# Low parts of the first layer's weight pieces: VectorE alone instead of VectorE and GpSimd by turns

## The chip, the core and the metric

The program runs on one core of one Trainium2 chip. The metric is the device time of that core in microseconds (us), the median of three runs. The engines are called as the profile calls them: PE (TensorE), PEld (its weight loads), DVE (VectorE), ACT (ScalarE), POOL (GpSimd) and SP (SyncE, which here issues most transfers).

## What is computed

The reference is a decoder trunk of two layers on 256 tokens of width 2048, all in float32. Each layer has three parts:

```
h = rmsnorm(x, g_mix_pre)
rq, rk, rv, rg, su, dq, dk, dv = split(h @ w_in)
x += rmsnorm(concat(retention(rq, rk, rv, rg), s5(su), diff_attention(dq, dk, dv)) @ w_out)
x += rmsnorm(cross_attention(rmsnorm(x), rmsnorm(mem)))
x += rmsnorm(square(relu(rmsnorm(x) @ w_up)) @ w_down)
```

The change touches only the first of these lines of the first layer: the products that make rv, rg, rq, rk and su.

## The kernel before

**Split products.** The float32 products are made of matmuls on a rounded format. A weight piece of 128 x 1024 numbers (512 KB) is loaded as `raw`; ACT rounds it into `hi` (L172); the rest, `raw - hi`, is the second part `lo` (L176). The activations `hT` are split in the same way. A product is hi x hi, lo x hi and hi x lo: for the pieces of `w_ina` that is twelve matmuls a piece on L264, L265 and L266, of which L265 reads `lo`; for those of `w_inb` 24 shorter ones on L329, L330 and L331.

**Stages of the first layer.** The projections run in the order RV, RG, RQ, RK (eight pieces each, `proj_A`) and SU (two groups of four pieces, `proj_B`), 40 pieces in all. In the profile RG starts at 43.28 us, SU at 155.2, and the last matmul of SU is out at 197.6. The numbers in tile names rise with the program's order. Piece 1 of RG is hi_459 with lo_460, the last piece of RQ is hi_942 with lo_943, the first of RK hi_977 with lo_978, and SU starts at hi_1265. `raw` has three buffers, `hi` and `lo` five each (`NRAW, NHL = 3, 5`).

**Other work of the same stretch.** While PE goes through these pieces, DVE also makes the parameters of both layers (`params`: L386 to L527, among them the powers and rotations of `cmul`, L473 to L478), the rotation table (L579 to L584), the S5 operands, and the elementwise parts of the projections (L986 to L992 is the rotation of rq and rk, L1053 and L1054 the gate of rg). `s5_setup` makes the S5 operands in eight units. For each unit DVE writes the block `BJ` (L633 to L640) and the block `C5` (L656 to L664); PE transposes BJ (L647, four matmuls) and multiplies by C5 (L672, eight records); ACT copies the results; DVE adds a diagonal (L682). BJ is one buffer in `ws`: DVE may write the next unit's BJ when PE and ACT have read the last one. `t5` uses POOL for integer work (L865).

**Order of the work.** The Tile framework orders each engine's instructions by priority, which is the place in the program, when it builds the kernel; on the chip each engine takes them in that order and waits where an operand is missing. `high_priority(offset=50)` moves an instruction 50 places ahead of its own. In the first layer's stretch up to the end of SU, `lo_pool` is 2 (`LOP = (2, 0)`), so `fetch` gives every second `lo` to POOL; elsewhere it is 0 and all `lo` are on DVE with no offset.

Of the kernel before, what the change touches and what calls it, by code (L numbers as in the profile page):

```python
# [8 lines left out]
F32 = mybir.dt.float32  # L9
# [4 lines left out]
ALU = mybir.AluOpType  # L14
AX = mybir.AxisListType
PSUM = bass.MemoryType.PSUM
DRAM = bass.MemoryType.DRAM

P = 128
# [29 lines left out]
class Trunk:  # L49
    def __init__(self, ctx, tc, ins, out):  # L50
        self.ctx, self.tc, self.nc, self.i, self.out = ctx, tc, tc.nc, ins, out
        self.bg = []
        self.first = None
        self.have = []
        self.count = 0
        self.lo_pool = 0
        self.todo = self.plan()
        self.uid = 0
        self.queue = 0
# [41 lines left out]
    # ------------------------------------------------------------ setup  # L101
# [10 lines left out]
    def rstd(self, out, ss, scale, n):  # L112
        """out[P, n] = (ss * scale + eps) ** -0.5"""
        nc = self.nc
        m = self.tmp.tile([P, 4], F32, tag="tiny", name=self.nm("ms"), bufs=8)
        nc.vector.tensor_scalar(m[:, 0:n], ss, scale, EPS, ALU.mult, ALU.add)  # L116
        nc.gpsimd.tensor_tensor(out=out, in0=m[:, 0:n], in1=self.mhalf[:, 0:n], op=ALU.pow)  # L117
# [5 lines left out]
    # ------------------------------------------------- split helpers  # L123
    def split_act(self, hi, lo, src):
        """hi = f32r(src), lo = f32r(src - hi)"""
        self.nc.scalar.copy(out=hi, in_=src)
        self.nc.vector.tensor_tensor(out=lo, in0=src, in1=hi.bitcast(F32), op=ALU.subtract)

    def plan(self):
        """the weight pieces in the order in which the products take them: (array, index)"""  # L130
        for l in range(L):
            def chunk(n, c, kps, *pre):
                return [(n, (l, *pre, c, k)) for k in kps]
            for c in (C_RV, C_RG, C_RQ, C_RK):
                yield from chunk("w_ina", c, range(8))
            for half in range(2):
                groups = [] if half else [G_SU, G_SU + 1]
                for g in groups + [G_DQ + 2 * half, G_DQ + 2 * half + 1, G_DK + 2 * half, G_DK + 2 * half + 1]:
                    yield from chunk("w_inb", g, range(4))
                yield from chunk("w_ina", C_DV + half, range(8))  # L140
            for ks in (self.KO, self.KD):
                for c in range(2):
                    yield from chunk("w_out", c, ks)
            for c in (2, 3):
                yield from chunk("w_out", c, range(8))
            for n in ("w_xk", "w_xq"):
                for c in range(2):
                    yield from chunk(n, c, range(4))
            yield from chunk("w_xv", 0, range(8))
            for c in range(4):  # L150
                yield from chunk("w_xo", c, range(2))
            for sc in range(4):
                for g in range(8):
                    yield from chunk("w_up", 8 * sc + g, range(4))
                for c in range(4):
                    yield from chunk("w_down", c, range(8), sc)

    def fetch(self):
        """load and split the next weight piece"""
# [3 lines left out]
        src = self.i[key[0]]  # L163
# [7 lines left out]
        with self.tc.high_priority(offset=50 if self.lo_pool else 0):  # L171
            self.nc.scalar.copy(out=hi, in_=raw)  # L172
        self.count += 1
        eng = self.nc.gpsimd if self.lo_pool and self.count % self.lo_pool == 0 else self.nc.vector
        with self.tc.high_priority(offset=50 if self.lo_pool else 0):
            eng.tensor_tensor(out=lo, in0=raw, in1=hi.bitcast(F32), op=ALU.subtract)  # L176
# [12 lines left out]
    def T8(self, slot, shape, dt=F32R, name="t"):  # L189
        """one of the eight 8 KB slots for transposed activations"""  # L190
        return self.tp.tile(shape, dt, tag=f"T{slot}", name=self.nm(name), bufs=1)
# [4 lines left out]
    def scale_split(self, hT, j, ts_, src, gcol):  # L196
        """hT[j][:, :, :, ts_] = f32r parts of src [P, 4, n] times the gain columns"""
# [6 lines left out]
    def from_T(self, hT, srcT, gcol, room=None):  # L204
        """hT from a feature-major input [P, 16, 256]"""
# [7 lines left out]
    def build_T(self, hT, src, t, j, gcol):  # L213
        """hT[j][:, :, :, tok tile t] from src [P tok, 512] times the gain columns"""
# [7 lines left out]
    def after(self, dst, src):  # L222
        """a load into dst starts only when src is there"""
# [6 lines left out]
    def begin(self):  # L230
        """the parameters, and x once its transpose is there"""
# [11 lines left out]
    def x_stat(self, t):  # L243
        """rstd [P, 1] of x tile t"""
# [12 lines left out]
    # ------------------------------------------------- projections  # L257
    def mm_A(self, a, lhs, kp, w, t, first, last):
        """a[tok tile t, 512] += h @ piece kp"""
# [11 lines left out]
    def proj_A(self, lhs, nk, wap, c, sink, arg=None, kps=None, lag=(0, 0)):  # L271
        """acc[tok, 2, 512] = h @ chunk c of w; lag = how many pieces tile 1 runs behind
        tile 0 at the start and at the end (then sink is called per tile)"""
# [33 lines left out]
    def proj_B(self, rhs, nk, wap, c, sink, arg=None, split=False, halves=False):  # L307
        """[P feat, 2 tiles, 256 tok] = group c of w, transposed, times h^T; split: all of token tile 0
        before token tile 1; halves: the products with the two parts of h side by side"""
# [44 lines left out]
    # ------------------------------------------------- trig  # L354
    def sincos(self, ang, n, sn, cs, wk):
        """sn, cs = sin(ang), cos(ang) of [P, n] fp32 angles of any size; wk(k) gives scratch"""
# [25 lines left out]
    def exp_small(self, out, a, wk):  # L382
        """out = exp(a), to fp32 rounding, a clamped to [-87, 88]"""
# [13 lines left out]
    # ------------------------------------------------- parameters of both layers  # L397
    def params(self):
        """rope tables, S5 discretisation (both layers, [P=(2g,64p), 32=(l,pair)])"""
# [19 lines left out]
        if True:  # L419
# [42 lines left out]
            # powers a^0..a^4 of a = mag e^{i th}: pw[P, m, 32]  # L462
# [23 lines left out]
            # unit rotation per chunk of four, and its doublings  # L486
# [11 lines left out]
            # f = (a - 1) / lambda  # L498
# [16 lines left out]
            # lambda of the differential heads  # L515
# [16 lines left out]
    # ------------------------------------------------- S5 operands of one layer, left in DRAM  # L532
# [5 lines left out]
    def s5_setup(self, l, gate=None):  # L538
# [24 lines left out]
        # rotation tables  # L563
# [28 lines left out]
        # B-bar; its imaginary part, like that of the state, is kept negated  # L592
# [11 lines left out]
        # units of two pairs of groups  # L604
# [22 lines left out]
        def stage_a(u):  # L627
            # a^{3-j} B-bar, block-diagonal over the two groups of a pair
# [21 lines left out]
        def stage_x(u):  # L650
            # C a^m, block-diagonal as well
# [14 lines left out]
        def stage_c(u):  # L666
            nc.scalar.copy(out=wtm[u % 2][:, 0:512], in_=pss[u])
            # B C a^m, the same for every j
# [5 lines left out]
        def stage_d(u):  # L674
            # shifted into the lower-triangular block Toeplitz operand; the skip on its diagonal
# [26 lines left out]
    # ------------------------------------------------- S5 group  # L702
    def su_sink(self, acc, arg):
        """[P, 2, 256] -> [P, 2, 4 j, 64 c]"""
# [5 lines left out]
    def s5_relayout(self, suP):  # L710
        """su channel-major -> U4 [(j, 2g, 16h), pair, chunk]"""
# [9 lines left out]
    def s5_main(self, l, st):  # L721
# [52 lines left out]
        def emit(u):  # L774
# [8 lines left out]
            # gelu (tanh form)  # L783
# [22 lines left out]
        # back to channel-major: gF[(q,2g,16h), ft, (i, c)]  # L806
# [34 lines left out]
    # ------------------------------------------------- T5 bias, left in DRAM as 8*bias + mask  # L841
    def t5(self):
        """steps over the bucket edges times the differences of the table's rows"""
# [46 lines left out]
    # ------------------------------------------------- differential heads  # L890
# [11 lines left out]
    def diff_heads(self, l, srcs, yds):  # L902
# [64 lines left out]
        # head -> tick of its four steps  # L967
# [9 lines left out]
    # ------------------------------------------------- retention  # L977
# [78 lines left out]
    # ------------------------------------------------- residual after a sub-layer  # L1056
    def post_sink(self, acc, arg, t0, t1):
        """y*g into self.y, partial sums of squares"""
# [13 lines left out]
    def residual(self, t, rfix=None):  # L1072
        """x tile t += y*g*rstd(y)"""
# [29 lines left out]
    def stat_of(self, t, gate=None):  # L1103
        """1 / rms of x tile t"""
# [7 lines left out]
    def row_of(self, dst, cols):  # L1112
        """dst[P, 256] = the two columns [P, 1] along the free axis of every partition"""
# [9 lines left out]
    # ------------------------------------------------- memory  # L1123
# [15 lines left out]
    # ------------------------------------------------- cross attention  # L1139
# [4 lines left out]
    def scaled(self, acc, arg):  # L1144
        """times a row [P, 256] that is the same on all partitions"""
# [66 lines left out]
    def proj_xo(self, l, xyT):  # L1212
        """four chunks of two pieces; tile 1 runs behind tile 0"""
# [20 lines left out]
    # ------------------------------------------------- MLP  # L1234
# [42 lines left out]
    # ------------------------------------------------- one layer  # L1277
    def layer(self, l, hT):
# [6 lines left out]
        self.lo_pool = self.LOP[l]  # L1285
        self.nt = tk[0]
        with ExitStack() as mx:
# [44 lines left out]
            self.lo_pool = 0  # L1332
# [17 lines left out]
            with ExitStack() as df:  # L1350
# [8 lines left out]
                # out-projection of the first two chunks over what is ready  # L1359
# [70 lines left out]
    LOP = (2, 0)  # L1430
# [55 lines left out]
def layouts(x):  # L1486
    """the inputs laid out as the program reads them, and arrays that depend on the shapes alone"""
# [6 lines left out]
    def tile_a(w):  # L1494
        # [..., K, N] -> [..., N/512, K/256, 128, 2, 512]
# [5 lines left out]
    def tile_b(w):  # L1501
        # [..., K, N] -> [..., N/256, K/512, 128, 4, 256]
# [21 lines left out]
    # persistent small things  # L1524
# [9 lines left out]
    # parameters that only the set-up reads  # L1534
# [12 lines left out]
    # S5: b [(g p), re/im, pair, h], c [(g p), re/im, pair, h]  # L1547
# [32 lines left out]
```

## Time and profile before

| what | us |
|---|---|
| median of three runs (2574.57 to 2579.67) | 2578.06 |
| span of the profiled execution | 2586.3 |
| PE busy in the span | 2494.8 |
| DVE busy | 1631.0 |
| ACT busy | 1226.0 |
| POOL busy | 179.7 |

The profile gives the profiled execution by its span, first to last instruction; a time of that same execution around the span is not given. The span is 8.2 us (0.32%) above the median of the runs. The share of busy time is an average over stages; the stretch from 43 to 198 us is where the change lies, and its own rows stand further down. A row's duration runs to the end of the instruction, which overlaps with the start of the next one; the cost of an instruction on a busy engine is the step from its start to the next start.

### The profile page before, as it was taken

How to read it: one execution, taken by the hardware profiler on the slowest of the kernel's cores; microseconds unless marked ns; L12 is line 12 of the kernel's file. 1: busy time of each engine (PE TensorE's matmuls, PEld its weight loads, DVE VectorE, ACT ScalarE, POOL GpSimd, SP SyncE). 2: the span in 40 equal slices, each digit the busy share in tenths (PEclk: the TensorE clock that was granted, in tenths of full speed). 3: DMA queues.
4: the chain of work that ended last, by engine and by line, in shares of the span. 5: the costliest groups of instructions: out<-in, count | busy, mean ns of one | idle time of the engine just before them, and what ended most of it. 6: DMA issues, size and time to landing. Idle time of an engine off the chain costs nothing.

```text
span 2586.3 us, 36202 instructions
## 1 busy us (share of the span) xinstructions
PE 2494.8 (96%) x13696; PEld 2143.4 (83%) x13696; DVE 1631.0 (63%) x2688; ACT 1226.0 (47%) x1936; POOL 179.7 (7%) x202
## 2 busy tenths in 40 slices
PE   6789999999999999999999999999999999999998
PEld 4588877898888888888878999879788888888886
DVE  8876766657876655555566586656665555555555
ACT  5443456656554434434445435556554444443443
POOL 3433310001000000000000001000000000000000
PEclk9889999999999999999999999999999999999999
DMA  6556665655666665566566555575465556656554
GB/s 247 190 193 190 212 190 166 210 173 172 214 215 212 187 195 187 187 195 187 188 201 197 178 182 177 171 223 177 132 196 193 189 187 195 188 187 195 187 188 146
DMA packets 145630, 491.49 MB, mean 190 GB/s; under 512 B 15744, under 2 KB 28032, under 8 KB 144176
## 3 DMA queue, kind: packets, MB, share of 16 engines
q1 hardware_dynamic: 139904, 470.47, 57.1%
q0 software_dynamic: 4976, 17.14, 2.1%
q8 instruction: 107, 1.75, 0.3%
q10 hardware_dynamic: 576, 1.57, 0.2%
q14 instruction: 67, 0.55, 0.1%
HBM read 469.20 MB, written 19.92 MB: 189 GB/s over the span
## 4 chain that ended last, share of the span: by engine, by line
PE 83%; DVE 7%; DMA 4%; issue 2%; ACT 2%; POOL 1%; SPq 0%; POOLq 0%; DVEq 0%; ACTq 0%
PE acc L326 18%; PE acc L264 13%; PE acc L266 13%; PE acc L265 13%; PE acc L327 9%; PE acc L329 3%; PE acc L330 3%; PE acc L331 3%; DVE lo L176 1%; DMA raw<-in_w_out_dram 1%; PE sm L218 1%; ACT hi L172 1%; DMA raw<-in_w_ina_dram 1%; DMA raw<-in_w_xk_dram 1%; PE sm L750 1%
## 5 line engine op out<-in xcount | busy, mean ns | idle before, releaser
L176 DVE TENSOR_TENSOR lo<-raw,hi 128x1024 fp32r<-128x1024 f32 x795 | 976.2, 1229 | 766.2 <-ACT hi L172 762.4
L172 ACT CAST hi<-raw 128x1024 fp32r<-128x1024 f32 x816 | 857.4, 1051 | 1089.2 <-PE acc L266 465.4
L326 PE MATMUL acc<-hm,hi 128*128 128x512 f32 x1984 | 700.2, 398 | 0.0
L327 PE MATMUL acc<-hm,lo 128*128 128x256 f32 x1984 | 557.0, 281 | 0.0
L326 PEld LDWEIGHTS acc<-hm,hi 128*128 128x128 f32 x1984 | 372.6, 188 | 91.3
L264 PE MATMUL acc<-hi,uT 128*128 128x512 f32 x1024 | 400.4, 391 | 1.6 <-DVE y L1252 1.6
L266 PE MATMUL acc<-hi,uT 128*128 128x512 f32 x1024 | 398.7, 389 | 0.0
L265 PE MATMUL acc<-lo,uT 128*128 128x512 f32 x1024 | 398.6, 389 | 0.0
L327 PEld LDWEIGHTS acc<-hm,lo 128*128 128x128 f32 x1984 | 374.8, 189 | 0.2
L264 PEld LDWEIGHTS acc<-hi,uT 128*128 128x128 f32 x1024 | 192.3, 188 | 41.8 <-DVE y L1252 2.4
L266 PEld LDWEIGHTS acc<-hi,uT 128*128 128x128 f32 x1024 | 192.2, 188 | 40.2
L265 PEld LDWEIGHTS acc<-lo,uT 128*128 128x128 f32 x1024 | 192.3, 188 | 39.2
L329 PE MATMUL acc<-hT,hi 128*128 128x256 f32 x640 | 185.2, 289 | 0.0
L330 PE MATMUL acc<-hT,hi 128*128 128x256 f32 x640 | 183.4, 287 | 0.0
L331 PE MATMUL acc<-hT,lo 128*128 128x256 f32 x640 | 183.2, 286 | 0.0
L265 PE MATMUL acc<-lo,hT 128*128 128x512 f32 x384 | 158.0, 411 | 15.5 <-POOL lo L176 7.9
L264 PE MATMUL acc<-hi,hT 128*128 128x512 f32 x384 | 157.9, 411 | 10.9 <-ACT hi L172 10.6
L266 PE MATMUL acc<-hi,hT 128*128 128x512 f32 x384 | 156.5, 408 | 3.6 <-DVE hT L202 3.6
L117 POOL TENSOR_TENSOR rs<-ms,mhalf 128x1 f32<-128x1 f32 x26 | 18.8, 725 | 1698.0 <-DVE ms L116 993.6
L330 PEld LDWEIGHTS acc<-hT,hi 128*128 128x128 f32 x640 | 123.9, 194 | 1.4
L329 PEld LDWEIGHTS acc<-hT,hi 128*128 128x128 f32 x640 | 123.5, 193 | 1.6 <-issue 1.0
L331 PEld LDWEIGHTS acc<-hT,lo 128*128 128x128 f32 x640 | 123.5, 193 | 1.5 <-issue 0.7
(403 smaller groups left out, 3191.9 us busy)
## 6 DMA issues: line engine op xcount, KB each, us to landing
raw<-in_w_up_dram SPq DMA_DIRECT2D x256, 512.0 KB, 3.5
raw<-in_w_down_dram SPq DMA_DIRECT2D x256, 512.0 KB, 3.5
raw<-in_w_ina_dram SPq DMA_DIRECT2D x96, 512.0 KB, 4.2
raw<-in_w_inb_dram SPq DMA_DIRECT2D x80, 512.0 KB, 4.1
raw<-in_w_out_dram SPq DMA_DIRECT2D x64, 512.0 KB, 4.2
pp<-s5d SPq DMA_DIRECT2D x16, 640.0 KB, 5.2
raw<-in_w_xk_dram SPq DMA_DIRECT2D x16, 512.0 KB, 4.2
raw<-in_w_xq_dram SPq DMA_DIRECT2D x16, 512.0 KB, 4.0
```

The source lines that it names most:

```text
L172: self.nc.scalar.copy(out=hi, in_=raw)
L176: eng.tensor_tensor(out=lo, in0=raw, in1=hi.bitcast(F32), op=ALU.subtract)
L218: nc.tensor.transpose(ps[:, q * P:(q + 1) * P], src[:, q * P:(q + 1) * P], self.ident)
L264: self.nc.tensor.matmul(a, lhsT=xh, rhs=hi[:, kk, :], start=first and kk == 0, stop=False)
L265: self.nc.tensor.matmul(a, lhsT=xh, rhs=lo[:, kk, :], start=False, stop=False)
L266: self.nc.tensor.matmul(a, lhsT=xl, rhs=hi[:, kk, :], start=False, stop=last and kk == 1)
L326: nc.tensor.matmul(acc[:, t, :], lhsT=hi[:, kk, cs], rhs=h, start=(k == 0), stop=False)
L327: nc.tensor.matmul(a, lhsT=lo[:, kk, cs], rhs=h[:, 0, :], start=False, stop=(k == nk - 1))
L329: nc.tensor.matmul(a, lhsT=hi[:, kk, cs], rhs=h[:, 0, :], start=(k == 0), stop=False)
L330: nc.tensor.matmul(a, lhsT=hi[:, kk, cs], rhs=h[:, 1, :], start=False, stop=False)
L331: nc.tensor.matmul(a, lhsT=lo[:, kk, cs], rhs=h[:, 0, :], start=False, stop=(k == nk - 1))
L750: nc.tensor.matmul(bu[:, r, a * 64:(a + 1) * 64], lhsT=win[:, a, r, :], rhs=U4[:, 2 * u + a, :], start=True, stop=True)
```

## The change

In the first layer, from RV to the end of SU, every `lo` is made on DVE. The flag `lo_pool` with its period becomes the flag `rush`, which only sets the priority: the offset of 50 stays for both halves of the split, now under one `with`. Comments and docstrings are blank lines or gone, so line numbers of the changed kernel are lower by 4 or 5 (L172 there is L176 here); below, in the text, all lines are those of the kernel before.

```diff
@@ __init__
-        self.count = 0
-        self.lo_pool = 0
+        self.rush = False
@@ fetch
-        with self.tc.high_priority(offset=50 if self.lo_pool else 0):
+        with self.tc.high_priority(offset=50 if self.rush else 0):
             self.nc.scalar.copy(out=hi, in_=raw)
-        self.count += 1
-        eng = self.nc.gpsimd if self.lo_pool and self.count % self.lo_pool == 0 else self.nc.vector
-        with self.tc.high_priority(offset=50 if self.lo_pool else 0):
-            eng.tensor_tensor(out=lo, in0=raw, in1=hi.bitcast(F32), op=ALU.subtract)
+            self.nc.vector.tensor_tensor(out=lo, in0=raw, in1=hi.bitcast(F32), op=ALU.subtract)
@@ layer
-        self.lo_pool = self.LOP[l]
+        self.rush = l == 0
...
-            self.lo_pool = 0
+            self.rush = False
@@ constants
-    LOP = (2, 0)
```

The scheduler sees the new engine, so the order of the rest moves too. Two places show it.

On DVE, at the first pieces of RG. Lines L473 to L478 (before) and L366 to L373 (change; there they are L370 to L377 of the kernel before) are parameter work. Before:

```order
L176 TENSOR_TENSOR lo_460<-raw_457,hi_459 128x1024
L473 TENSOR_TENSOR par_152<-pwr 128x32
L474 TENSOR_TENSOR par_152<-pwi 128x32
L475 TENSOR_TENSOR pwr<-par_152 128x32
L476 TENSOR_TENSOR par_152<-pwr,pwi 128x32
L477 TENSOR_TENSOR par_152<-pwi,pwr 128x32
L478 TENSOR_TENSOR pwi<-par_152 128x32
L473 TENSOR_TENSOR par_152<-pwr 128x32
L474 TENSOR_TENSOR par_152<-pwi 128x32
L176 TENSOR_TENSOR lo_535<-raw_532,hi_534 128x1024
```

With the change:

```order
L172 TENSOR_TENSOR lo_460<-raw_457,hi_459 128x1024
L368 TENSOR_TENSOR par_152<-par_152 128x160
L369 CAST par_152<-par_152 128x160
L172 TENSOR_TENSOR lo_495<-raw_492,hi_494 128x1024
L370 TENSOR_TENSOR par_152<-par_152 128x160
L371 SCALAR_TENSOR_TENSOR angb<-par_152 128x160
L172 TENSOR_TENSOR lo_535<-raw_532,hi_534 128x1024
```

lo_495, which POOL made before, now stands between its neighbours on DVE, and all three stand ahead of parameter work that they followed before.

On PE, around the first piece of RK. Before (sm_1035 is the transpose of the fourth S5 unit; those of the first three, sm_810, sm_885 and sm_960, stand further up, among the pieces of RQ):

```order
L266 MATMUL acc_757<-hi_942,hT_102 128x512
L647 MATMUL sm_1035<-pk,ws_598 128x128 x4
L264 MATMUL acc_757<-hi_942,hT_102 128x512
L265 MATMUL acc_757<-lo_943,hT_102 128x512
L266 MATMUL acc_757<-hi_942,hT_102 128x512
L264 MATMUL acc_757<-hi_942,hT_102 128x512
L265 MATMUL acc_757<-lo_943,hT_102 128x512
L266 MATMUL acc_757<-hi_942,hT_102 128x512
L264 MATMUL acc_1064<-hi_977,hT_99 128x512
L265 MATMUL acc_1064<-lo_978,hT_99 128x512
```

With the change (L643 and L668 are L647 and L672 of the kernel before):

```order
L262 MATMUL acc_757<-hi_942,hT_102 128x512
L260 MATMUL acc_1064<-hi_977,hT_99 128x512
L643 MATMUL sm_810<-pk,ws_598 128x128 x4
L668 MATMUL sm_838<-ws_598 128x128 x3
L668 MATMUL sm_838<-ws_598,ws_7_105 128x128
L643 MATMUL sm_885<-pk,ws_598 128x128 x4
L668 MATMUL sm_913<-c_119_772,ws_598 128x128 x3
L668 MATMUL sm_913<-c_119_772,ws_7_105 128x128
L261 MATMUL acc_1064<-lo_978,hT_99 128x512
```

The first two S5 units have moved from the middle of RQ to behind the first matmul of RK, ahead of the first matmul that reads lo_978.

## Rows read from the trace of the kernel before

**Rows 1.** First line of the page: the span.
```profile
span 2586.3 us, 36202 instructions
```

**Rows 2.** Windows: RG up to 68 us, RQ, RK, SU, and the rest.
```profile
core 0: us, PE busy (x) PEld busy (x) DVE busy (x) ACT busy (x) POOL busy (x), PEclk, DMA share, GB/s
43.28:68.00 24.72, 19.09 (x68) 14.64 (x69) 23.53 (x82) 14.08 (x27) 12.56 (x12) 0.86 0.63 228
68.00:100.00 32.00, 22.29 (x87) 16.95 (x85) 23.18 (x70) 13.34 (x24) 18.67 (x8) 0.84 0.51 169
100.00:155.20 55.20, 47.27 (x223) 38.47 (x224) 51.91 (x135) 27.89 (x67) 16.77 (x7) 0.91 0.56 183
155.20:197.60 42.40, 34.08 (x261) 33.65 (x259) 24.57 (x43) 17.30 (x40) 14.63 (x8) 0.88 0.65 220
200.00:2586.00 2386.00, 2343.26 (x12960) 2018.91 (x12960) 1472.77 (x2241) 1127.97 (x1732) 100.63 (x148) 0.99 0.60 188
```

**Rows 3.** Waits of PE up to 250 us: in total, times, longest.
```profile
PE sm L899 <- DVE st L992: 11.7, 2, 8.3
PE acc L265 <- POOL lo L176: 7.9, 2, 6.9
PE acc L265 <- DVE lo L176: 5.9, 4, 3.7
PE sm L647 <- DVE ws L639: 4.2, 2, 2.2
PE sm L1120 <- DVE ws L635: 2.8, 1, 2.8
```

**Rows 4.** Timeline of PE around 85 us: start, duration, instruction.
```profile
85.35 0.63 PE L266 MATMUL acc<-hi,hT 128*128 128x512 f32 x1
85.78 0.63 PE L264 MATMUL acc<-hi,hT 128*128 128x512 f32 x1
...
91.05 0.39 PE L265 MATMUL acc<-lo,hT 128*128 128x512 f32 x1
91.28 0.39 PE L266 MATMUL acc<-hi,hT 128*128 128x512 f32 x1
```

**Rows 5.** Groups of POOL: the low parts made there.
```profile
L176 POOL TENSOR_TENSOR lo<-raw,hi 128x1024 fp32r<-128x1024 f32 x21 | 61.3, 2922 | 80.2 <-ACT hi L172 69.2 <-DVE ws L635 5.8 <-PE sm L672 5.2
```

**Rows 6.** Timeline of POOL: two of its 21 low parts.
```profile
15.08 2.37 POOL L176 TENSOR_TENSOR lo<-raw,hi 128x1024 fp32r<-128x1024 f32 x1 [0.37 <-ACT hi L172]
...
74.07 10.63 POOL L176 TENSOR_TENSOR lo<-raw,hi 128x1024 fp32r<-128x1024 f32 x1 [5.53 <-ACT hi L172]
```

**Rows 7.** Timeline of DVE: one operation beside a POOL low part and alone.
```profile
15.14 2.35 DVE L391 TENSOR_SCALAR par<-par 128x32 f32<-128x32 f32 x1
...
25.64 0.17 DVE L391 TENSOR_SCALAR par<-par 128x32 f32<-128x32 f32 x1
```

**Rows 8.** Timeline of DVE: a low part and the instruction behind it.
```profile
43.36 1.22 DVE L176 TENSOR_TENSOR lo<-raw,hi 128x1024 fp32r<-128x1024 f32 x1
44.49 0.18 DVE L473 TENSOR_TENSOR par<-pwr 128x32 f32<-128x32 f32 x1
```

**Rows 9.** Timeline of DVE: idle time before 90.96, and the last stretched instruction.
```profile
90.96 1.23 DVE L176 TENSOR_TENSOR lo<-raw,hi 128x1024 fp32r<-128x1024 f32 x1 [8.45 <-ACT hi L172]
...
179.35 1.78 DVE L682 SCALAR_TENSOR_TENSOR c<-pk,c 128x128 f32<-128x128 f32 x2 [3.40 <-ACT c L679]
```

**Rows 10.** Timeline of DVE: steps of the rotation table and of an S5 unit.
```profile
72.91 0.42 DVE L579 TENSOR_TENSOR ws<-rt,rot 128x256 f32<-128x256 f32 x1
73.24 0.42 DVE L580 TENSOR_TENSOR ws<-rt,rot 128x256 f32<-128x256 f32 x1
...
113.27 0.33 DVE L656 TENSOR_TENSOR c<-ws,pwr 128x160 f32<-128x160 f32 x1
...
115.37 0.61 DVE L682 SCALAR_TENSOR_TENSOR c<-pk,c 128x128 f32<-128x128 f32 x2
...
117.75 0.33 DVE L656 TENSOR_TENSOR c<-ws,pwr 128x160 f32<-128x160 f32 x1
```

## The prediction
> **What bounds the kernel now.** I read the windows by stage first. From 200 us to the end PE is busy 2343.26 of 2386.00 us [rows 2], so that part is paced by PE, and whatever the first 200 us end earlier, the whole should end earlier. The order of PE and of the transfers behind SU is the same in both programs. In the four windows from the start of RG to the end of SU, PE is idle 5.63 + 9.71 + 7.93 + 8.32 = 31.6 us [rows 2], while DVE is busy 23.53 of 24.72, 23.18 of 32.00 and 51.91 of 55.20 us in the first three. The reader is to see that this is the one stretch where DVE, not PE, sets the pace.
>
> Second, the waits of PE say which work is late: the rotated rq and rk for L899 (11.7 us), a low part from POOL (7.9), one from DVE (5.9 in four waits, the longest 3.7), an S5 unit for L647 (4.2) and the block for L1120 (2.8) [rows 3]. All but the POOL one come from DVE. A wait costs more than itself: after the one of 6.9 us two matmuls of 512 columns start 0.43 us apart, where others start 0.23 apart [rows 4]. That is the step between the two levels of the clock, 1.2 and 2.4 GHz; the granted clock of the four windows is 0.86, 0.84, 0.91 and 0.88, against 0.99 later [rows 2]. From 85.35 to 91.05 us it issues 14 matmuls in 5.70 us, which at 0.23 would be 3.2: 2.5 us lost.
>
> Third, why DVE is late. The low part on POOL at 15.08 takes 2.37 us; the DVE instruction that starts beside it takes 2.35 us, and the same operation alone 0.17 [rows 6, 7]. The timeline of DVE has 18 such instructions, each beside one of POOL's 21 low parts: the first that is a small operation is the one of rows 7, the last the pair at 179.35, 1.78 us in place of 0.61 [rows 9, 10]. Over the 18, duration minus the duration of the same form alone comes to 35.4 us (15 of them lie between 1.7 and 2.7). So POOL's 61.3 us [rows 5] aren't free: DVE stands still for more than half of them. At two of the other three low parts DVE was out of work. At the third it goes the other way: the low part at 74.07 takes 10.63 us [rows 6], in which DVE goes through 22 instructions and then idles 8.45 us [rows 9]; PE's wait of 6.9 us is for this one.
>
> **The change part by part.** *Removed*: 21 low parts on POOL, with the 35.4 us that they hold DVE. *Added*: 21 low parts on DVE at a step of 44.49 - 43.36 = 1.13 us [rows 8], 23.7 us. DVE has 35.4 - 23.7 = 11.7 us less to do, before any wait that goes. POOL's remaining work of the stretch (integer steps, small powers, transfers that it issues) now starts no later. No transfer is added or taken away; on SP's queue the table and S5 stores stand one to three weight loads later, and the loads wait for their buffers anyway.
>
> *Waits that go.* POOL's low part: 7.9. DVE's 3.7 at 60.93 us, for a low part that stands behind three instructions stretched by 6.9 us together: without them it's in time. L647: 4.2, both behind a stretched instruction. L899: 11.7; DVE comes to it earlier, and PE later, since its place is now a piece or more further on. Together 27.5 us. Behind five of these waits PE runs at the lower clock: 2.5 us at the longest but one, less at the shorter ones; I take 2.2 on the mean, 11 us. Sum that can go: 38.5 us. The wait for L1120 I leave standing: its block stands behind more low parts now, but its place on PE moved ahead as well.
>
> *Waits that come.* The order on DVE has no low part between lo_943 (last of RQ) and lo_978 (first of RK), but 72 instructions: 24 of 256 columns at 0.33, two S5 units at 117.75 - 113.27 = 4.5 each less one L682 at 0.5, and smaller ones, about 2.5 us [rows 10]: together 19 us. PE meets lo_978 with its second matmul of RK. If lo_943 is made as early as the five buffers allow, some four and a half pieces ahead (a piece is 12 x 0.23 = 2.8 us, [rows 4]), PE has 12.6 us of matmuls left and waits 19 + 1.1 - 12.6 = 7.5 us. If lo_943 is only just in time, one piece ahead, PE waits 17. The moved L647 and L672 lie inside this wait and shorten it a little. I take 7, the near end, because DVE has 11.7 us less to do while the pieces are as many, and add 2.5 for the clock behind it: 9.5. Then the S5 units: BJ is one buffer, so DVE waits for PE's L647 and PE for DVE's next unit. A missed hand-off costs 2.1 (4.2 in two, [rows 3]) plus 2.2 for the clock; none to eight of them, 0 to 34 us. In the order each unit's L640 stands a low part or two ahead of PE's need, so I take less than one, 3 us.
>
> Sum: 38.5 - 9.5 - 3 = 26 us. The profiled execution would go from 2586.3 [rows 1] to 2560.3 us; that span stands 8.2 us above the median of the runs, so against the median 2578.06 - 26 = **2552 us**.
>
> *Rules weighed.* The Trainium skill, Perfetto Trace Analysis (Optimizing Scalar/DVE Operations), says that where DVE is saturated it may help to give some of its work to GPSIMD, which speaks against this change, and adds that the two share a port, so that it might not. By its first half the change would end as rival C below; the rows of stretched instructions agree with the second. The Trainium skill, SBUF — State Buffer (SBUF: two separate sides), says of that port that whichever starts first has it for the whole instruction. By this POOL would wait for one DVE instruction of 0.4 us; the low part of 10.63 us waited through 22 of them, so the measurement goes further than the rule. If the rule were right there and that wait had another cause, the 6.9 + 2.5 us might stay, and the time would be 2561.
>
> **The rivals.** *B, the hand-offs eat it.* Place: L647 and L672 on PE against L633 to L640 on DVE from the start of RK on. The engines have less slack there than before, since four units that lay within RQ are now within RK. For it: L647 waited twice before [rows 3]. Against: both times behind a stretched instruction. At six missed hand-offs of eight, 26 us, the change is worth 38.5 - 9.5 - 26 = 3 us: 2575. It gets a 0.13 chance; of that 0.02 is still faster, 0.01 slower.
>
> *C, DVE is simply overloaded.* Place: DVE's queue ahead of lo_978. If the stretched instructions have a cause that stays (the transfers, say), nothing of the 35.4 us comes back, and DVE, busy 98.6 of the 111.9 us up to 155.2 [rows 2], gets 23.7 us more. It would come to lo_978 about 24 us later than I have it, PE would wait there for all of that, and the end would move by it: 2578 + 24 = 2602 us. Between 26 us gained with 35.4 back and 24 lost with none, the point from which it decides is about 17 us back, half. Against it: all stretched instructions lie beside a low part of POOL, and by about its length. 0.07.
>
> That the change doesn't do what it says is excluded by the order: 21 low parts left POOL and stand on DVE.
>
> **How the numbers follow.** The forecast has 0.80, all of it faster. What a measurement of this kernel can tell from no change is 0.2%, 5.2 us. Faster: 0.80 + 0.02 = 0.82. Same: the 0.10 left of B. Slower: 0.07 + 0.01 = 0.08. The range: at the lower end all of PE's 31.6 us of idle time and the 11 us of clock go and nothing comes, 42.6 us: 2535. At the upper end lo_978 costs 17 + 2.5 and four hand-offs 17: 38.5 - 36.5 = 2 us, 2576, just beyond B. Outside lie C and the tails of the forecast, less than 2 in 10.
>
> **What would show it.** Right: no DVE instruction of 2 us or more up to 200 us; DVE busy in the first 155 us about 10 us less; no wait of PE for L899 above 2 us; the last matmul of SU near 172 us in place of 197.6, and PE from there on as before. A wait of PE of 5 to 17 us for lo_978 near 90 us. Wrong: small operations of 2 us still on DVE (C); PE's waits for L647 and L672 of more than 10 us in all (B); or an early end of SU that is lost again before 600 us, which would mean that the later part isn't paced by PE.

## The result and the profile after

| | time, us | ratio to before, 95% interval |
|---|---|---|
| before | 2577.19 median of 4 (2574.57 to 2579.67) | |
| changed | **2550.57** median of 4 (2548.09 to 2555.70) | 0.9893 [0.988, 0.9906] |

The change makes the kernel 26.6 us faster; the forecast was 2552. The profiled execution of the changed kernel took 2548.09 us, with a span of 2546.3. Line numbers of the changed kernel are mostly 4 or 5 lower (L176 is L172, L265 is L261, L647 is L643, L672 is L668, L1120 is L1116, L780 is L776); those ahead of the split's second half are 1 lower (L172 is L171, L126 is L125). Each experiment has line numbers of its own.

The windows of [rows 2] in the changed kernel, the last one now with its end at 2546:

```profile
43.28:68.00 24.72, 23.33 (x103) 18.97 (x102) 18.12 (x70) 15.81 (x33) 3.76 (x4) 1.00 0.76 281
68.00:100.00 32.00, 21.13 (x88) 17.16 (x89) 30.04 (x109) 10.97 (x18) 5.58 (x7) 0.84 0.35 115
100.00:155.20 55.20, 50.49 (x319) 44.48 (x318) 53.67 (x152) 34.26 (x83) 0.00 (x0) 0.97 0.65 215
155.20:197.60 42.40, 40.90 (x311) 39.03 (x310) 24.60 (x45) 16.56 (x30) 6.80 (x10) 0.96 0.81 277
200.00:2546.00 2346.00, 2310.97 (x12751) 1985.44 (x12751) 1455.38 (x2215) 1120.08 (x1723) 95.70 (x139) 1.00 0.56 189
```

PE's idle time in the first, third and fourth window falls from 5.63, 7.93 and 8.32 us [rows 2] to 1.39, 4.71 and 1.50, and the granted clock rises there; the second, 68 to 100 us, has 10.9 us idle in place of 9.7 and stays at 0.84. A window in time no longer holds the same work, so I compare up to a point of the program from here on: the first product on L780, which reads U, behind SU ("the first product of U" below; L750 reads U too and starts 2.4 us ahead of it in both kernels). Before, in lines by source (the first number behind the durations is its first start):

```profile
L780 PE MATMUL sm<-U,pp x64: 217/275/323, 222.8 to 1542.1; 128*128 128x64 f32 x64
```

and after:

```profile
L776 PE MATMUL sm<-U,pp x64: 217/275/323, 196.1 to 1505.7; 128*128 128x64 f32 x64
```

It comes 26.7 us earlier, all of what the medians differ by. The windows from 0 to that point (columns as in [rows 2]), before:

```profile
0.00:222.80 222.80, 173.82 (x919) 146.43 (x920) 170.80 (x466) 105.20 (x212) 82.79 (x63) 0.91 0.62 210
```

and after:

```profile
0.00:196.10 196.10, 165.68 (x920) 142.16 (x921) 159.07 (x487) 104.89 (x212) 22.46 (x42) 0.95 0.69 239
```

DVE has 21 instructions more and is busy 11.7 us less. Where it comes from is seen by kind of instruction, in the groups of DVE up to 200 us. Before:

```profile
L640 DVE TENSOR_TENSOR ws<-ws,ws 64x128 f32<-64x128 f32 x16 | 8.4, 528 | 0.3 <-issue 0.3
L656 DVE TENSOR_TENSOR c<-ws,pwr 128x160 f32<-128x160 f32 x8 | 4.8, 600 | 0.2
```

After, the same two lines and the low parts:

```profile
L172 DVE TENSOR_TENSOR lo<-raw,hi 128x1024 fp32r<-128x1024 f32 x52 | 63.3, 1220 | 20.1 <-ACT hi L171 19.8
L636 DVE TENSOR_TENSOR ws<-ws,ws 64x128 f32<-64x128 f32 x16 | 4.5, 282 | 0.0
L652 DVE TENSOR_TENSOR c<-ws,pwr 128x160 f32<-128x160 f32 x8 | 2.6, 326 | 0.7 <-DMA rotd<-rt 0.5
```

The same small operations take half their former mean. What PE still waits for up to that point, other than the start (in total, times, longest):

```profile
PE sm L1116 <- DVE ones L1115: 8.8, 1, 8.8
PE sm L668 <- DVE ws L659: 3.2, 1, 3.2
...
PE acc L261 <- DVE lo L172: 2.1, 2, 1.6
PE sm L668 <- ACT ws L644: 1.9, 2, 1.4
...
PE sm L668 <- DVE c L659: 0.9, 1, 0.9
...
PE sm L643 <- issue: 0.3, 1, 0.3
```

Against [rows 3] the rotated rq and rk and POOL's low parts are gone, and the wait for the block of ones has grown from 2.8 to 8.8 us. All its waits together, start included, were 48.7 us and are 30.1. The timeline of PE shows where the remaining large ones stand, between the end of RG and the first matmul of RK that reads lo_978:

```profile
66.22 0.39 PE L262 MATMUL acc<-hi,hT 128*128 128x512 f32 x1
75.37 0.79 PE L1116 MATMUL sm<-ones 128*128 128x128 f32 x2 [8.76 <-DVE ones L1115]
...
95.23 0.71 PE L643 MATMUL sm<-pk,ws 128*128 128x128 f32 x4 [0.29 <-issue]
99.15 0.92 PE L668 MATMUL sm<-ws 128*128 128x128 f32 x6 [3.21 <-DVE ws L659]
...
101.66 1.15 PE L668 MATMUL sm<-c,ws 128*128 128x128 f32 x8 [0.93 <-DVE c L659]
104.39 0.80 PE L261 MATMUL acc<-lo,hT 128*128 128x512 f32 x1 [1.59 <-DVE lo L172]
```

### The profile page after: what moved, and what is told of

It is laid out like the page before. It is cut to its first block, busy times and chain, and to the rows that moved or that the text cites. A ratio compares the mean times of both kernels' runs of the same rounds, so it can differ in the third digit from the quotient of the medians.

```text
span 2546.3 us, 36190 instructions
## 1 busy us (share of the span) xinstructions
PE 2480.1 (97%) x13696; PEld 2130.7 (84%) x13696; DVE 1618.4 (64%) x2709; ACT 1226.2 (48%) x1936; POOL 120.8 (5%) x181
## 4 chain that ended last, share of the span: by engine, by line
PE 79%; DMA 4%; DVE 4%; ACT 3%; issue 2%; POOL 1%; DVEq 0%; POOLq 0%; ACTq 0%
PE acc L322 18%; PE acc L260 13%; PE acc L262 13%; PE acc L261 13%; PE acc L323 9%; PE acc L325 3%; PE acc L326 3%; PE acc L327 3%; DVE lo L172 1%; DMA raw<-in_w_out_dram 1%; ACT hi L171 1%; DMA raw<-in_w_ina_dram 1%; DMA raw<-in_w_xk_dram 1%; PE sm L214 1%; ACT junk L120 1%
## 5 line engine op out<-in xcount | busy, mean ns | idle before, releaser
L172 DVE TENSOR_TENSOR lo<-raw,hi 128x1024 fp32r<-128x1024 f32 x816 | 997.6, 1224 | 756.9 <-ACT hi L171 754.0
L171 ACT CAST hi<-raw 128x1024 fp32r<-128x1024 f32 x816 | 857.9, 1052 | 1084.7 <-PE acc L262 482.0
L261 PE MATMUL acc<-lo,uT 128*128 128x512 f32 x1024 | 398.6, 389 | 0.0
L261 PEld LDWEIGHTS acc<-lo,uT 128*128 128x128 f32 x1024 | 192.3, 188 | 39.1
L261 PE MATMUL acc<-lo,hT 128*128 128x512 f32 x384 | 154.5, 402 | 3.7 <-DVE lo L172 3.6
```

Source lines behind the costliest of these rows:

```text
L172: self.nc.vector.tensor_tensor(out=lo, in0=raw, in1=hi.bitcast(F32), op=ALU.subtract)
L261: self.nc.tensor.matmul(a, lhsT=xh, rhs=lo[:, kk, :], start=False, stop=False)
```

## The experiments

Theory A: POOL's subtraction holds DVE, and the change is worth what DVE no longer stands still. Rival C: the stretched rows have another cause, and the change gains by what POOL did late. What stayed open besides: whether the new wait for the ones is a loss of its own, and whether the place of the low parts in the order matters.

**POOL works again, for nobody (e1_shadow).**

```diff
+            if self.rush:
+                self.count += 1
+                if self.count % 2 == 0:
+                    self.nc.gpsimd.tensor_tensor(out=self.shadow, in0=raw.rearrange('p a b -> p (a b)'), in1=hi.rearrange('p a b -> p (a b)').bitcast(F32), op=ALU.subtract)
```

> The changed kernel plus 21 extra subtractions on POOL (raw minus hi, the same form as the low parts that POOL made before) into a scratch tile that nobody reads; every low part is still made on DVE. Nothing of the computation is left out. Theory A (POOL's subtraction holds DVE's small operations): DVE again has some 15 instructions of 1.7 us or more up to 200 us that take 0.2 to 0.6 alone, in all some 35 us of DVE; PE's waits for DVE up to 200 us grow by 20 to 30 us; time 2570 to 2585 us against 2551 for the changed kernel, as no low part of DVE has gone. Theory C (the stretched instructions had a cause that stays, and POOL only made its low parts late): the scratch tile is waited for by nobody, no new stretched rows, 2549 to 2554 us.

Measured: 2584.8 us, ratio to before 1.0029 [1.0018, 1.004]: 34 us slower than the changed kernel, and slower than before. Timeline of POOL, then of DVE, in this kernel:

```profile
29.53 2.39 POOL L177 TENSOR_TENSOR shadow<-raw,hi 128x1024 f32<-128x1024 f32 x1
32.21 2.47 POOL L177 TENSOR_TENSOR shadow<-raw,hi 128x1024 f32<-128x1024 f32 x1 [0.29 <-POOL shadow L177]
```

```profile
29.60 2.37 DVE L394 SCALAR_TENSOR_TENSOR par<-par 128x32 f32<-128x32 f32 x1
...
32.05 0.18 DVE L394 SCALAR_TENSOR_TENSOR par<-par 128x32 f32<-128x32 f32 x1
...
32.39 2.34 DVE L394 SCALAR_TENSOR_TENSOR par<-par 128x32 f32<-128x32 f32 x1
```

The operation that takes 0.18 alone takes 2.34 and 2.37 beside a subtraction that nobody waits for as data. The window to the first product of U:

```profile
0.00:225.70 225.70, 170.93 (x919) 144.83 (x920) 201.06 (x487) 104.75 (x212) 86.23 (x63) 0.91 0.61 207
```

With the same 487 instructions DVE is busy 201.06 in place of 159.07 us, 42.0 us more, and the point comes 29.6 us later; the rest of the 34 us comes behind it. C has fallen.

**POOL busy, but only writing (e2_memset).**

```diff
-                    self.nc.gpsimd.tensor_tensor(out=self.shadow, in0=raw.rearrange('p a b -> p (a b)'), in1=hi.rearrange('p a b -> p (a b)').bitcast(F32), op=ALU.subtract)
+                    self.nc.gpsimd.tensor_copy(self.shadow[:, 0:1], hi[:, 0, 0:1].bitcast(F32))
+                    self.nc.gpsimd.memset(self.shadow, 0.0)
+                    self.nc.gpsimd.memset(self.shadow, 1.0)
```

> The same as e1_shadow, but in place of each subtraction POOL copies one column of hi (so that it starts at the same moment) and then fills the scratch tile twice with a constant: it writes 128x1024 and reads nothing. Nothing of the computation is left out. If any work of POOL holds DVE (theory A1), there are rows of DVE stretched by the length of the fill and the time rises by about as much per us of POOL work as in e1_shadow. If only POOL instructions that read two operands hold DVE (theory A2), no DVE instruction is stretched beside a fill and the time is 2549 to 2554 us. I hold A2 likelier, since POOL's fills at the start of the kernel before show no stretched row beside them.

Measured: 2552.8 us, ratio 0.9901 [0.9886, 0.9915], not to be told from the changed kernel.

```profile
0.00:196.40 196.40, 163.59 (x919) 139.75 (x920) 160.91 (x487) 104.67 (x212) 81.76 (x105) 0.96 0.71 238
```

POOL is busy 81.76 us in this window, about as long as before the change, and DVE only 1.8 us longer than without it. So it is not a busy POOL that costs. Still, the expectation that no DVE row is longer beside a fill failed. Rows with two inputs in SBUF keep their length there, but at four places (12.59, 27.59, 45.00 and 163.17 us) a TENSOR_SCALAR row, with one input, is held, and what stands right behind it with it. The clearest of the four, POOL and then DVE:

```profile
27.51 0.95 POOL L179 MEMSET shadow<- 128x1024 f32 x1
```

```profile
27.59 0.97 DVE L373 TENSOR_SCALAR par<-angb 128x160 int32<-128x160 f32 x1
```

and the same operation in the changed kernel, with no fill:

```profile
27.98 0.23 DVE L366 TENSOR_SCALAR par<-angb 128x160 int32<-128x160 f32 x1
```

At 45.00 us POOL's column copy and a transfer that it issues stand there as well, so the cause of that one is open. The four places are enough for the 1.8 us. The one-column copies show the other direction. POOL's timeline, a copy of 128 elements and the fill behind it:

```profile
83.94 0.20 POOL L177 COPY shadow<-hi 128x1 f32<-128x1 f32 x1
...
88.70 6.05 POOL L177 COPY shadow<-hi 128x1 f32<-128x1 f32 x1 [2.53 <-ACT hi L172]
94.82 0.95 POOL L178 MEMSET shadow<- 128x1024 f32 x1
```

DVE in the same stretch, where each row starts ahead of the end of the one before, up to 94.72:

```profile
94.23 0.28 DVE L642 TENSOR_TENSOR ws<-ws 64x128 f32<-64x128 f32 x1
94.44 0.27 DVE L643 TENSOR_TENSOR ws<-ws,ws 64x128 f32<-64x128 f32 x1
94.72 0.29 DVE L642 TENSOR_TENSOR ws<-ws 64x128 f32<-64x128 f32 x1
```

**POOL reads one operand (e7_copy).** The same with `tensor_copy(self.shadow, hi)`, whole, in place of the subtraction.

> As e1_shadow, but POOL copies hi into the scratch tile (one operand read in place of two, 128x1024, 21 times). Nothing of the computation is left out. If a POOL instruction holds DVE only where it reads two operands, there are no stretched rows and the time is that of the changed kernel, 2548 to 2555 us. If reading one is enough, DVE rows beside a copy are as long as the copy, and the time lies between the 2553 us of the fills and the 2585 us of the subtractions, by the copy's length: 2560 to 2580 us. I hold the second likelier, since the one-column copies of e2_memset took 0.2 us when DVE was idle and up to 6.05 us when it was not: they wait for DVE, so they share something with it.

Measured: 2559.8 us, ratio 0.9934 [0.9918, 0.995], 9 us slower than the changed kernel. POOL, then DVE:

```profile
128.60 1.17 POOL L177 COPY shadow<-hi 128x1024 f32<-128x1024 f32 x1 [2.85 <-ACT hi L172]
```

```profile
128.38 0.28 DVE L640 TENSOR_TENSOR ws<-ws 64x128 f32<-64x128 f32 x1
...
128.87 1.03 DVE L640 TENSOR_TENSOR ws<-ws 64x128 f32<-64x128 f32 x1
```

Reading one operand is enough: DVE is held for about the copy's 1.0 us. Another copy of this run, POOL and then DVE:

```profile
133.90 1.20 POOL L177 COPY shadow<-hi 128x1024 f32<-128x1024 f32 x1 [4.14 <-ACT hi L172]
```

```profile
133.91 0.28 DVE L634 TENSOR_TENSOR ws<-ws,pwj 128x128 f32<-128x128 f32 x1
134.11 1.13 DVE L635 TENSOR_TENSOR ws<-ws,pwj 128x128 f32<-128x128 f32 x1
```

Here the held row starts ahead of the end of the one before it (133.91 + 0.28 = 134.19).

**Half as many (e6_fourth).** The kernel before with `LOP = (4, 0)` in place of `(2, 0)`.

> The kernel before with every fourth low part of the stretch on POOL in place of every second (10 in place of 21). Same computation. If each low part on POOL costs its share (theory A: 35 us of DVE in 18 stretched instructions, less 1.13 us for each that moves to DVE), there are 8 to 10 stretched instructions and the time is 2560 to 2570 us, about midway between 2577 and 2551. If the loss was the one low part of 10.63 us and its wait of 6.9 us alone, the time is 2551 to 2556 or 2574 to 2580 us, by whether such a case still occurs, and not midway.

Measured: 2564.8 us, ratio 0.9952 [0.9934, 0.9969], 12.4 us below before and 14.2 above the changed kernel: midway. So the loss is spread over the low parts, not in the one of 10.63 us [rows 6].

The doses side by side, up to the first product of U and to the end (the runs of before beside the experiments had medians of 2576.6 and 2577.3 us):

| POOL's extra work | first product of U | DVE busy until then | median |
|---|---|---|---|
| none (changed) | 196.1 | 159.07 | 2550.6 |
| 21 column copies, 42 fills (e2) | 196.4 | 160.91 | 2552.8 |
| 21 copies (e7) | 202.0 | 173.87 | 2559.8 |
| 21 subtractions (e1) | 225.7 | 201.06 | 2584.8 |
| 10 low parts, and 10 fewer on DVE (e6) | 210.6 | 169.69 | 2564.8 |
| 21 low parts, and 21 fewer on DVE (before) | 222.8 | 170.80 | 2577.2 |

Each subtraction holds DVE for (201.06 - 159.07) / 21 = 2.0 us on the mean, each copy for 0.7, a pair of fills with its column for 0.09. Taking a low part off DVE saves 1.13. With that, a low part on POOL held DVE (170.80 - 159.07) / 21 + 1.13 = 1.7 us in the kernel before and (169.69 - 159.07) / 10 + 1.13 = 2.2 us in e6. DVE's busy time alone does not give the point: e6 and the kernel before differ by 1.1 us in it and by 12.2 us at the point. The kernel before also loses 7.9 us in PE's waits for POOL's low parts themselves [rows 3], e6 only 1.0.

**The wait for the ones (e3_ones, e9_early).** e3 moves the line `self.row_of(self.row, self.r_x)` behind the projections RQ and RK, e9 ahead of RG.

> The changed kernel with the row that SU needs (two blocks of ones times a column on DVE, two small products on PE) made behind the projections RQ and RK in place of ahead of them. Same computation. If the wait of 8.8 us of PE for that block stood on the path by itself, as the change's one loss, PE has no wait of more than 3 us at that place and the time is 2541 to 2546 us (8.8 us and up to 2.5 us of matmuls at the lower clock, less a new wait of up to 3 behind RK). If DVE's chain up to the first low part of RK is what binds, the wait only moves to that low part, grows there by 5 to 9 us, and the time stays 2549 to 2553 us.

> The changed kernel with the row that SU needs made ahead of the projection RG, some 100 matmuls earlier, in place of ahead of RQ. Same computation. PE's wait of 8.8 us for the block of ones goes in either case. If that wait stood on the path by itself, 2540 to 2546 us. If DVE's queue up to the first low part of RK binds (as e3_ones suggests), PE waits there by 6 to 9 us more than the 6.0 of the changed kernel and the time is 2548 to 2553 us.

Measured: 2553.5 us, 0.9902 [0.9886, 0.9918], and 2548.7 us, 0.9888 [0.9874, 0.9901]. Neither differs from the changed kernel by more than the intervals. The timeline of PE in e3_ones, its waits from the end of RG on:

```profile
74.46 0.50 PE L261 MATMUL acc<-lo,hT 128*128 128x512 f32 x1 [2.59 <-DVE lo L172]
94.74 1.08 PE L643 MATMUL sm<-pk,ws 128*128 128x128 f32 x4 [7.49 <-issue]
98.31 1.62 PE L668 MATMUL sm<-ws 128*128 128x128 f32 x6 [2.49 <-DVE ws L659]
104.20 0.50 PE L261 MATMUL acc<-lo,hT 128*128 128x512 f32 x1 [1.28 <-DVE lo L172]
```

Without the 8.76 us PE comes earlier to the S5 unit and waits there; the first matmul on lo_978 starts at 104.20, and at 104.39 in the changed kernel. In e9 it is 104.03. The wait for the ones and those ahead of lo_978 are one debt, and the time at which DVE gets to lo_978 sets it.

**The order on DVE (e4_noprio, e13_early150, e10_both).** e4: priority offset 0 in place of 50. e13: e9 with 150. e10: e9 with `PAUSE = 12` in place of 8.

> The changed kernel with the high and low parts of the stretch in the order in which they are written (priority offset 0 in place of 50). Same computation. If the change gains because POOL no longer holds DVE, and the order on DVE is second to that, the time is 2547 to 2558 us, and DVE's idle time for hi between 43 and 68 us (6.6 us in the changed kernel, at places where a low part stands in the queue ahead of its hi) becomes less. If the gain hangs on the low parts being ahead on DVE, PE waits for low parts by 10 us or more in all and the time is 2560 us or above.

> e9_early with the low parts further ahead on DVE (priority offset 150 in place of 50): the first low part of RK stands 46 instructions behind the last of RQ in place of 75. Same computation. DVE has as much to do up to the end of RK as in e9_early (it was busy 31.18 of 32.00 and 53.28 of 55.20 us there). If DVE's sum binds, the order only chooses where PE waits and the time is 2546 to 2554 us; if the place of the low parts binds, PE's waits from 68 to 110 us (12.2 us in e9_early) fall below 6 and the time is 2540 to 2545 us. After e10_both I hold the first likelier.

> e9_early with the set-up of the S5 units started 4 ticks later (a pause of 12 ticks in place of 8): on DVE the first low part of RK then stands 38 instructions behind the last of RQ in place of 75, and the units reach into SU, where DVE was busy 24.60 of 42.40 us. Same computation. If DVE's queue there is what bound the changed kernel and e3_ones, PE's waits from 68 to 110 us (14.8 us in the changed kernel) fall to 5 or less and the time is 2536 to 2543 us. If PE then waits for the S5 units within SU or at its end as much, 2547 to 2553 us.

Measured: 2558.4 us, 0.9928 [0.9912, 0.9944]; 2557.4 us, 0.9918 [0.9903, 0.9933]; 2557.4 us, 0.9917 [0.9901, 0.9932]. All three lose some 7 us; e10 and e13 lie outside both of the ranges that were expected of them. e4 does not lose its part in the stretch: the first product of U starts at 194.1 us there. DVE is busy 18.45 us from 43.28 to 68 us, against 18.12, so that its idle time hardly fell (6.3 against 6.6), and that part of the expectation was wrong. It loses most of it later, in a wait that the changed kernel doesn't have (e4, waits of PE from 225 to 700 us):

```profile
PE sm L824 <- ACT gw L125: 7.0, 1, 7.0
```

The kernel before had 3.5 us of the same wait in its first profile and 1.6 in its second; why the order of the first layer's low parts moves it I didn't try. e10 has its first product of U at 189.4 us, 6.7 earlier than the changed kernel, and gives that back in the next 50 us: its window behind that point,

```profile
189.40:225.00 35.60, 30.33 (x212) 27.02 (x213) 30.82 (x61) 12.74 (x22) 13.32 (x14) 0.95 0.48 164
```

leaves PE idle for 5.3 us, where the same stretch of the changed kernel,

```profile
196.10:232.00 35.90, 34.15 (x256) 30.71 (x255) 30.56 (x70) 14.46 (x25) 18.74 (x16) 1.00 0.58 179
```

has 1.8, and the first matmul acc<-hi,hT behind it starts at 242.06 and 242.42. Where e10 then loses the 7.8 us by which its span is longer I didn't follow. e13 moves PE's wait to its S5 unit (8.7 us at 94.89) and to the rotated operands (4.7, which were gone). Its first product of U is at 196.5, so up to there they cost nothing on balance; it loses 4.6 us between there and that matmul, at 247.40.

**Less work on DVE (e11_actput).**

```diff
+            if l == 0:
+                v.tensor_tensor(out=t[0], in0=t[0], in1=t[1], op=ALU.subtract)
...
+                if l == 0:
+                    nc.scalar.copy(out=BJ[h, :, 0, :, g, :], in_=t[0][h])
...
+                    continue
                 v.tensor_tensor(out=BJ[h, :, 0, :, g, :], in0=t[0][h], in1=t[1][h], op=ALU.subtract)
```

This stands on top of e9. The other three sums of each half (of BJ and of the C block) are changed in the same way.

> e9_early with less work on DVE in the S5 units of the first layer: the two sums of a block are made once over 128 partitions, in place of twice over 64, and ACT copies their halves into the padded blocks. DVE has 4 instructions fewer in each of 8 units, at steps of 0.20 and 0.24 us, 7 us in all; ACT has 8 small copies more in each, some 15 us, and each unit one hand-off more between engines. Same computation. If DVE's sum binds, 2541 to 2546 us (7 us less, less a hand-off or two of 1 us). If the hand-offs of the units cost as much as DVE saves, 2547 to 2555 us.

Measured: 2562.2 us, 0.9936 [0.992, 0.9952], slower than the changed kernel by 12 us and outside what either case was expected to give. DVE is busy 150.25 us up to the first product of U, 8.8 less, yet that point comes only 2.0 us earlier. Behind it the span loses 16 us, of which a wait of PE for gw is 5.6; the rest isn't located. So less work on DVE alone did not bring the end forward. That its order and the hand-offs of the units bind the changed kernel fits this, but isn't shown: e11 also gives ACT 64 copies and each unit a hand-off more.

**A second profile of before (before_again).**

> The kernel before, unchanged, for a second profile. The spans of the two profiles at hand differ by 40.0 us (2586.3 and 2546.3) and the medians by 26.6. If the profiled execution of before was a disturbed one (its clock was 0.986 against 0.988 to 0.991 in the other runs of it), this one has a span of 2572 to 2578 us, its first 200 us are those of the first profile within 2 us, and the difference lies behind them. If instead its first 200 us are shorter by some 10 us, the change gained less in this stretch than the two profiles say.

Measured: 2575.6 us.

```profile
span 2573.5 us, 36202 instructions
```

```profile
L780 PE MATMUL sm<-U,pp x64: 217/275/323, 222.3 to 1533.9; 128*128 128x64 f32 x64
```

The first stretch repeats to 0.5 us. The first profile of before had lost 12.3 us more behind it, so the 40.0 us between the first two spans are 26.7 of the change and 13.3 of that execution, for a cause that stays open; against this profile the span is 27.2 us shorter.

## Why the prediction was right

- *DVE is stretched, 35.4 us in 18 instructions; 21 low parts add 23.7; net -11.7.* Measured -11.7 (170.80 to 159.07). e1_shadow shows the cause. Up to 200 us the longest DVE row of the changed kernel is a low part of 1.23 us. The reading that all stretched rows lie beside low parts was not quite right: in the kernel before two more, of 1.07 and 1.04 us at 156.73 and 159.54, lie beside POOL's integer steps on L865, and the changed kernel keeps three of about 1.0 us beside the same steps (67.69, 70.37, 79.26). That is the same effect, of a POOL that still does some work.
- *Waits that go, 27.5.* All four went: no wait for rotated rq and rk, for POOL's low part or for L647's unit; the 3.7 too. Not in my sum: PE's waits up to 43 us also fell, from 15.8 to 11.9, mainly that for hT at L202 (3.6 to 0.3). I had begun at RG.
- *"The wait for L1120 I leave standing."* This is the term that was mis-sized: 8.8 in place of 2.8, because the block stands behind more work on DVE than I allowed for.
- *lo_978 costs 7.* The sign that was named, one wait of 5 to 17 us for lo_978 near 90 us, did not come: the wait for lo_978 itself is 1.59 us, at 104.39. The four waits from 95.23 to 104.39, which all stand ahead of it or at it, sum to 6.0. With the ones it is 14.8, of which I had 9.8. By e3_ones and e9_early the two are one, so the split was not mine to make: what I needed was the time at which DVE gets to lo_978. The range's far end, 17, was for this one wait and would have covered both.
- *S5 hand-offs, 3.* Two more waits (ACT's ws), of 1.9 us together. Rival B's 26 did not come.
- *Clock.* PE's waits fell by 48.7 - 30.1 = 18.6 us; the point moved by 26.7; the 8.1 between are PE's busy time (173.82 to 165.68), matmuls at the lower clock, where I had 11 less 2.5, and a part of the 3 us for the hand-offs. A row of this: the clock of RG went from 0.86 [rows 2] to 1.00.
- *PE from there on as before.* What lies behind the first product of U is 2573.5 - 222.3 = 2351.2 us in the second profile of before and 2546.3 - 196.1 = 2350.2 after. The last matmul of SU starts at 169.59 in place of 197.60; I said near 172.
- *DVE busy about 10 us less in the first 155 us.* As I put it this was wrong (132.50 to 135.97), since the same time now holds more work; to the same point of the program it is right.

The total was nearer than its terms, and that was luck: 14.8 - 9.8 = 5.0 us too little for DVE's arrival at lo_978 were largely made up by the 3.9 us of the start that I had left out.

The Trainium skill, SBUF — State Buffer (SBUF: two separate sides), says that a DVE operation with two inputs in SBUF contends only with a GpSimd operation that reads SBUF. The rows with two inputs agree: beside the fills of e2_memset they keep their length, and beside a copy or a subtraction one of them is held. Its lock for one instruction does not cover what the waiting side saw: 6.05 us for a copy of 128 elements. The Trainium skill, Perfetto Trace Analysis (Optimizing Scalar/DVE Operations), says that a busy DVE may gain by giving work to GPSIMD, and that it might not, for the shared port. The first half goes against the 26.6 us gained here by taking that work back; e1_shadow agrees with the second.

## What to carry to other kernels

Before work goes from DVE to POOL, look at the DVE instruction that runs beside a POOL instruction of that kind, and compare it with the same form alone: here a low part moved to POOL saved DVE 1.13 us and held it 1.7 in the kernel before and 2.2 in e6. Work that POOL only writes (fills) can stay there: 42 fills and 21 columns cost DVE 1.8 us together. When several waits lie ahead of one late instruction, price the arrival of that instruction and not the waits, and test a shift by where the time goes afterwards: five reorderings moved PE's waits, and none beat the plain change by more than a measurement tells.

## What the runs showed of the hardware

POOL's fills of 128x1024, at 0.95 us each, ran beside DVE's rows with two inputs without a stretched one; a copy held such a row about 1.0 us and a subtraction about 2.35. For these rows not POOL's business but its reading counts. A row with one input, TENSOR_SCALAR, was held by a fill too (0.97 in place of 0.23 us at 27.59 in e2_memset).

In the other direction a POOL instruction that reads can wait through a dense run of DVE's rows. In e2_memset the column copy waited from 88.70 to 94.75, and the first DVE row that does not start ahead of its predecessor's end is the one at 94.72. The low part of 10.63 us [rows 6] fits that: before the change, DVE's rows overlap from 74.07 on until DVE goes idle at 90.96 - 8.45 = 82.51 [rows 9], and POOL ends 2.2 us later, at 84.70. It was a wait behind a dense run of DVE, not slow work. An end of the overlap isn't always needed: the copy at 133.90 in e7_copy got in behind one row of 0.28 us, with the next one overlapping it. What decides how long POOL waits stays open.
